# Four column groups of the first block's input projection as plain float32 products with raw weights

## The chip, the cores and the metric

The kernel runs on one core of one Trainium2 chip. The metric is device time in microseconds (us) of one execution; lower is better. TensorE (PE) multiplies, with its weight loads listed apart as PEld; VectorE (DVE), ScalarE (ACT) and GpSimd (POOL) work on elements; SyncE (SP) issues most DMAs.

## The reference, cut to what matters

A sequence of 256 tokens with 1024 channels passes two layers of a first block and then two layers of a second block. The change touches the input projection of the first block:

```
for l in range(2):
    h = rmsnorm(x, norm_mix[l])
    proj = einsum('bsd,de->bse', h, w_in[l])          # 1024 x 3476, float32
    m_q, m_k, m_v, m_o, m_i, m_f, b_q, ..., n_g = split(proj)
    qk = silu(causal_conv(concat([m_q, m_k]), conv_qk[l]))
    y = concat([mlstm(...), moba(...), nsa(...)])     # three mixers of the tokens
    x = x + y @ w_out[l]
    x = x + square(relu(rmsnorm(x, norm_ffn[l]) @ w_ff1[l])) @ w_ff2[l]
```

The groups in question are m_q, m_k, m_v and m_o, 512 columns each: the inputs of the mLSTM mixer. Its two convolved inputs (m_q, m_k) are made in two halves of heads.

## The kernel before

All weights go through one stream (class `Stream`) in the order of their use. A unit is up to 1072 float32 values on each of 128 partitions, mostly 128 x 1024 (512 KB). SP loads it into one of four raw buffers. Then `conv` splits it: ACT copies raw to `whi` (float32r, L154), and POOL (every second unit) or DVE subtracts `wlo` = raw - whi (L156). Up to four units are split ahead of use. The activations are split alike: `xT` transposes x (L570), ACT writes `xh` (L576) and DVE `xl` (L579), both times the gain of the norm. A product is then three float32r matmuls in one PSUM bank, xh.whi + xh.wlo + xl.whi (`mm3`, L242 is the line of every `mm`).

The first block's projection of one layer runs in this order: a group of 268 columns, one of 128, one of 512, the compression weights, one of 520, and then the four groups of the change in the order "0o1v": the first halves of m_q and m_k ("0": two pairs of column blocks, weights stationary, 256 tokens moving, `wpair`), m_o ("o": tokens on partitions, 512 columns moving, `xchunk`), the second halves ("1"), and m_v ("v"). After a pair, `conv_tile` runs the causal convolution: one DVE multiplication (L1151), one ACT copy (L1035) and three DVE instructions (L1037) for each block of 128 columns.

Attention work runs beside the projections. Two lanes hold queues of generator tasks (NSA, MoBA, gates, later mLSTM). Each `mm` adds its modelled time to a counter; at each 1000 ns (`tick`) the weight stream is converted ahead and every lane makes one step. The order on each engine is then settled by the framework, which reorders instructions by a simulated timeline. The tasks' own matmuls (scores, P @ v) and transposes have plain float32 operands. When "1" is done, three ticks later `act_conv` applies the tanh set and queues the mLSTM tasks (`mlstm_task`), which run beside "v" and the first products with w_out. `outproj` takes the mixers' results in the order n, b, m0, m1.

At the end of the feed-forward part, `bound_half` adds the result to x for one half of the columns, transposes it and computes the next norm, while the held products of the other half still run. DVE lines that the prediction names belong to the attention tasks: L296 to L299 (rope), L811 to L814 (compression, `cmph`), L861 and L866 (gains of the NSA norm), L714 (copy of transposed probabilities), L1019 (gates), L1086 (the mLSTM output `w`).

Of the kernel before, what the change touches and what calls it, by code (L numbers as in the profile page):

```python
# [31 lines left out]
C_SB = 1152         # [s, t]: NEG where t <= s  # L32
C_TRI = 1280        # -1 where s' >= s
C_COS = 1408        # [2, 16]
C_SIN = 1440        # [2, 16]
C_CM = 1472         # compressed mask, additive [2, 16]
C_CM1 = 1504        # compressed mask, 0/1 [2, 16]
C_SUM = 1536        # row sums of the hi/lo pairs, 16 wide
C_KBD = 1552        # [32, 2]
C_VBD = 1554        # [64, 4]  # L40
C_S8 = 1558         # [40, 8]
C_MONE = 1566       # -1
C_ONE = 1567        # 1
C_DUP = 1568        # [r, c] = 1 where c = r modulo 64
C_N = 1696
# [69 lines left out]
class Stream:  # L115
    """The weights in the order of use: loaded, then split into two float32r parts."""
    RAW = 4
    BUFS = 5
    SUB = 1072
# [9 lines left out]
    def add(self, a, b, *dmas):  # L129
        self.units.append((a, b, dmas))  # L130

    def load(self):
        u = self.n_load
        self.n_load += 1
        a, b, dmas = self.units[u]
        t = self.k.wraw.tile([128, self.SUB], F32, name="raw", tag="raw")
        v = t[:, :a * b].rearrange("p (a b) -> p a b", a=a)
        for f, src in dmas:
            self.k.nc.sync.dma_start(f(v), src)
        self.raw[u] = v  # L140

    def conv(self):
# [5 lines left out]
        a, b, _ = self.units[u]  # L148
        v = self.raw.pop(u)
        hi = self.k.wsub.tile([128, self.SUB], F32R, name="whi", tag="whi")  # L150
# [22 lines left out]
class K:  # L173
# [37 lines left out]
    def steps(self):  # L211
        """One step of every lane, and what was put off until now."""
# [44 lines left out]
    def rstd(self, out, ssq, inv, n, tag, lane="", ssq2=None, token=None):  # L257
        """out = 1 / sqrt(ssq * inv + EPS), or with two parts of the mean: 1 / sqrt(ssq + ssq2 + EPS)."""
# [30 lines left out]
    def rope(self, x, nh, lane, eng=None):  # L289
        """x [128, 2, nh, >=16] in place on the first 16."""  # L290
# [11 lines left out]
    def setup(self):  # L302
        nc, A = self.nc, self.A
        self.x = self.cst.tile([128, 2, DM], F32, name="x")
        cp = self.cst.tile([128, C_N], F32, name="cp")
        self.cp = cp
        wz = self.cst.tile([128, 512], BF16, name="wz")
# [18 lines left out]
        self.xl = self.cst.tile([128, KT, 256], F32R, name="xl")  # L326
        self.rs = self.cst.tile([128, 2], F32, name="rs")
# [5 lines left out]
        nc.sync.dma_start(cp[:, 128:], A["consts"][:, 128:])  # L333
# [6 lines left out]
    def setup2(self):  # L340
        nc, A, cp = self.nc, self.A, self.cp
        st = self.big.tile([128, 2048], F32, name="qkT", tag="qkT")
        cr = st[:96, 0:128]
        for i, n in enumerate(("norm_ffn", "pre_norm_2")):
# [25 lines left out]
        nc.vector.tensor_copy(self.msb, cp[:, C_SB:C_SB + 128])  # L370
        self.s8 = self.cst.tile([128, 8], F32R, name="s8")
        nc.scalar.activation(self.s8, cp[:, C_S8:C_S8 + 8], AF.Copy)
        self.tri = self.cst.tile([128, 129], F32R, name="tri")
        nc.scalar.activation(self.tri[:, 0:128], cp[:, C_TRI:C_TRI + 128], AF.Copy)
        nc.scalar.activation(self.tri[:, 128:129], cp[:, C_MONE:C_MONE + 1], AF.Copy)
        self.zero = self.cst.tile([8, 256], F32, name="zero")
        nc.gpsimd.memset(self.zero, 0.0)
        self.cumr = self.cst.tile([128, 384], F32R, name="cumr")
        nc.gpsimd.memset(self.cumr.bitcast(F32), 0.0)
        self.negM = self.cst.tile([64, 256], F32R, name="negM")  # L380
        nc.gpsimd.memset(self.negM.bitcast(F32), 0.0)
# [16 lines left out]
    def plan(self):  # L398
# [4 lines left out]
        def cols(t, l, width, c0, n, kts):  # L403
            for k0 in range(0, KT, kts):
                w.add(kts, n, (same, dram(t, (l * DM + k0 * 128) * width + c0, [[width, 128], [128 * width, kts], [1, n]])))

        def xch(t, l, width, c0, n):
            cols(t, l, width, c0, n, 2)
# [5 lines left out]
        for l in range(2):  # L414
            t, W = A["w_in"], 3476
            cols(t, l, W, 3208, 268, 2 if l == 0 else 4)
# [8 lines left out]
            for step in self.ORDER:  # L425
                if step == "o":
                    xch(t, l, W, 1536, 512)
                elif step == "v":
                    xch(t, l, W, 1024, 512)
                else:  # L430
                    for c in (0, 512):
                        cols(t, l, W, c + 256 * int(step), 256, 4)
# [34 lines left out]
    def xchunk(self, n, evac, first=None, pieces=None, both=False):  # L467
        """x @ n columns, tokens on partitions; first: the flag of the norm before, whose halves may still be due."""
# [36 lines left out]
    def wpair(self, ps, first=None):  # L505
        """ps[j] [128, 256] = (x @ weight columns)^T for two blocks of 128 columns."""
        k = 0
        while k < KT:
# [976 lines left out]
```

## Time and profile before

| what | value |
|---|---|
| time, median of 3 runs | 1159.69 us (1158.9 to 1159.82) |
| span of the profiled execution, first to last instruction | 1157.1 us |
| mean granted clock of TensorE | 0.986 of 2.4 GHz |
| busy: PE, PEld | 1110.5 us, 964.6 us |
| busy: DVE, ACT, POOL | 683.7, 639.4, 453.7 us |
| ACT copies raw to whi | 328, 344.4 us |
| subtractions on POOL, on DVE | 164, 408.8 us; 164, 214.4 us |

The profile is one execution. Its own time on the device stands nowhere beside its span; the median of the runs is 2.6 us longer than the span, which is what lies around it. Busy times are sums of instructions, and they overlap between engines; a long busy sum of an engine costs time only where another engine waits for it.

### The profile page before, as it was taken

The page shows a single profiled execution, that of the slowest core. Times are in us where ns is not written, and L with a number is a line of the kernel's source. Part 1 is how long each engine was busy: PE and PEld are TensorE (multiplying, and loading weights), DVE is VectorE, ACT ScalarE, POOL GpSimd, SP SyncE. Part 2 cuts the span into 40 slices and gives each one's busy share as a digit, 9 for nine tenths or more (in the row PEclk, how much of TensorE's full clock was granted, in tenths as well). Part 3 has the DMA queues.
Part 4 walks back from the last instruction along what each step waited for, and adds up shares of the span by engine and source line. Part 5 has one row for each costly group of instructions (what it writes and reads, how often), then busy time and mean ns, then how long its engine had stood idle before and what let it go on. Part 6 is the DMA issues. An engine that isn't in the chain of part 4 may idle for free.

```text
span 1157.1 us, 18183 instructions
## 1 busy us (share of the span) xinstructions
PE 1110.5 (96%) x6839; PEld 964.6 (83%) x6839; DVE 683.7 (59%) x1319; ACT 639.4 (55%) x1213; POOL 453.7 (39%) x234
## 2 busy tenths in 40 slices
PE   6988989999999999999999999999999999999997
PEld 4876878998998787878989898797997877979986
DVE  3897866545456896766555655474364386623543
ACT  4665546544556555546454545666655466676452
POOL 4652323444443442323444443434442243353421
PEclk8998999999999998999999999999999999999999
DMA  7743244656565633344665555644353346444530
GB/s 224 236 138 100 98 130 146 200 182 195 180 198 157 202 110 104 116 128 155 193 192 188 184 184 162 186 127 145 109 185 108 127 146 185 146 126 113 180 127 36
DMA packets 115511, 177.88 MB, mean 154 GB/s; under 512 B 5808, under 2 KB 75776, under 8 KB 115424
## 3 DMA queue, kind: packets, MB, share of 16 engines
q1 hardware_dynamic: 114368, 174.14, 47.9%
q0 software_dynamic: 832, 2.51, 0.9%
q8 instruction: 53, 0.87, 0.3%
q14 instruction: 34, 0.28, 0.1%
q10 hardware_dynamic: 224, 0.08, 0.0%
HBM read 175.66 MB, written 1.05 MB: 153 GB/s over the span
## 4 chain that ended last, share of the span: by engine, by line
PE 50%; DVE 3%; ACT 1%; issue 0%; DVEq 0%
PE g L242 34%; PE a L242 14%; PE a L710 1%; DVE wlo L156 1%; PE a L754 0%; DVE mc L272 0%; ACT w L1220 0%; ACT whi L154 0%; DVE rsm L271 0%; PE a L1247 0%; DVE rsm L263 0%; DVE w L1229 0%; DVE gate L1402 0%; DVE gate L1377 0%; ACT L275 0%
## 5 line engine op out<-in xcount | busy, mean ns | idle before, releaser
L156 POOL TENSOR_TENSOR wlo<-raw,whi 128x1024 fp32r<-128x1024 f32 (+2 forms) x164 | 408.8, 2493 | 637.5 <-ACT whi L154 519.8
L154 ACT ACTIVATE whi<-raw 128x1024 fp32r<-128x1024 f32 (+2 forms) x328 | 344.4, 1054 | 295.6 <-PE g L242 185.8
L156 DVE TENSOR_TENSOR wlo<-raw,whi 128x1024 fp32r<-128x1024 f32 (+2 forms) x164 | 214.4, 1308 | 156.0 <-ACT whi L154 144.9
L242 PE MATMUL g<-whi,xl 128*128 128x512 f32 (+3 forms) x480 | 174.8, 368 | 1.6 <-DVE xl L579 1.6
L242 PE MATMUL g<-wlo,xh 128*128 128x512 f32 (+3 forms) x480 | 175.3, 367 | 1.0 <-POOL wlo L156 0.7
L242 PE MATMUL g<-whi,xh 128*128 128x512 f32 (+2 forms) x480 | 174.3, 368 | 0.5 <-ACT xh L576 0.5
L242 PE MATMUL g<-whi,mh 128*128 128x512 f32 x416 | 163.7, 396 | 0.7 <-ACT mh L755 0.7
L242 PE MATMUL g<-wlo,mh 128*128 128x512 f32 x416 | 164.4, 395 | 0.0
L242 PE MATMUL g<-whi,ml 128*128 128x512 f32 x416 | 160.1, 394 | 0.3 <-DVE ml L756 0.3
L242 PE MATMUL a<-xl,whi 128*128 128x256 f32 x480 | 134.8, 281 | 0.0
L242 PE MATMUL a<-xh,wlo 128*128 128x256 f32 x480 | 134.5, 280 | 0.0
L242 PE MATMUL a<-xh,whi 128*128 128x256 f32 x480 | 134.4, 280 | 0.0
L242 PE MATMUL g<-xl,whi 128*128 128x256 f32 x432 | 123.8, 288 | 1.7 <-DVE xl L579 1.7
L242 PE MATMUL g<-xh,wlo 128*128 128x256 f32 x432 | 123.4, 286 | 0.8 <-DVE wlo L156 0.8
L242 PE MATMUL g<-xh,whi 128*128 128x256 f32 x432 | 123.3, 288 | 0.7 <-ACT xh L576 0.4
L678 DVE TENSOR_TENSOR ml<-e,mh 128x256 fp32r<-128x256 f32 x64 | 91.1, 1441 | 31.1 <-ACT mh L677 31.1
L242 PEld LDWEIGHTS g<-whi,xl 128*128 128x128 f32 x480 | 91.9, 192 | 17.8 <-issue 2.9
L242 PEld LDWEIGHTS g<-wlo,xh 128*128 128x128 f32 x480 | 92.0, 192 | 16.6 <-issue 2.2
L242 PEld LDWEIGHTS g<-whi,xh 128*128 128x128 f32 x480 | 91.5, 192 | 13.5 <-ACT xh L576 0.7
L242 PEld LDWEIGHTS g<-whi,ml 128*128 128x128 f32 x416 | 77.7, 188 | 17.6 <-DVE ml L756 0.5
L242 PEld LDWEIGHTS g<-whi,mh 128*128 128x128 f32 x416 | 78.1, 188 | 17.0 <-ACT mh L755 0.9
L242 PEld LDWEIGHTS a<-xl,whi 128*128 128x128 f32 x480 | 90.2, 188 | 1.3
(323 smaller groups left out, 1757.4 us busy)
## 6 DMA issues: line engine op xcount, KB each, us to landing
raw<-in_w_in_dram SPq DMA_DIRECT2D x130, 512.0 KB, 3.7
raw<-in_w_ff_dram SPq DMA_DIRECT2D x128, 512.0 KB, 3.9
raw<-in_w_out_dram SPq DMA_DIRECT2D x40, 512.0 KB, 3.3
raw<-in_w_in_dram SPq DMA_DIRECT2D x16, 520.0 KB, 4.2
raw<-in_cmp_w_dram SPq DMA_DIRECT2D x16, 256.0 KB, 3.8
raw<-in_w_in_dram SPq DMA_DIRECT2D x4, 268.0 KB, 12.2
raw<-in_w_in_dram SPq DMA_DIRECT2D x2, 536.0 KB, 3.9
x<-in_x_dram SPq DMA_DIRECT2D x4, 256.0 KB, 7.6
```

The costliest lines, as they stand in the source:

```text
L154: nc.scalar.activation(hv, v, AF.Copy)
L156: e.tensor_tensor(lv, v, hv.bitcast(F32), ALU.subtract)
L242: i = self.nc.tensor.matmul(out, l, r, start=st, stop=sp, skip_group_check=skip)
L678: nc.vector.tensor_tensor(ml[:, j], u, mh[:, j].bitcast(F32), ALU.subtract)
L710: nc.tensor.transpose(ps[:, b * 128:(b + 1) * 128], P[:, i, b * 128:(b + 1) * 128], self.ident)
```

## The change

A unit of the four groups is marked `whole`. `conv` passes it on raw, with no ACT copy and no subtraction, and its raw buffer stays occupied until PE has read it. Its products are single matmuls of plain float32 operands: the raw weights and a new operand `x32`, the transposed x times the gain in float32, which `xT` writes with extra ACT copies at the two norms that precede the first block's layers (flags "i" and "g0"). The counter of the ticks takes n / 0.6 ns (512 columns) or 430 ns (256) for such a product.

x32 needs 8 KB on each partition. To make room, units are at most 1040 values (the 268-column group of layer 1 becomes four units instead of two), 265 columns of the constants are loaded by a DMA on ACT's queue into a buffer used once (`once`), the rows of zeros are taken from other tiles (`zero`, `negM`), the warm-up operand `wz` and one lane's `sph` use other buffers' tags.

```diff
 class Stream:
-    SUB = 1072
+    SUB = 1040
...
     def conv(self):
...
+        if whole:
+            self.out[u] = (v, None)
+            return
...
 def setup(self):
-        cp = self.cst.tile([128, C_N], F32, name="cp")
+        cp = self.cst.tile([128, C_KEEP], F32, name="cp")
-        wz = self.cst.tile([128, 512], BF16, name="wz")
+        wz = self.big.tile([128, 512], BF16, name="y", tag="y", bufs=3)
+        self.x32 = self.cst.tile([128, KT, 256], F32, name="x32")
-        nc.sync.dma_start(cp[:, 128:], A["consts"][:, 128:])
+        nc.sync.dma_start(cp[:, 128:], A["consts"][:, 128:C_KEEP])
...
 def setup2(self):
+        once = st[:, 1280:1280 + C_N - C_KEEP]
+        nc.scalar.dma_start(once, A["consts"][:, C_KEEP:])
-        nc.vector.tensor_copy(self.msb, cp[:, C_SB:C_SB + 128])
+        nc.vector.tensor_copy(self.msb, once[C_SB])
-        self.zero = self.cst.tile([8, 256], F32, name="zero")
-        nc.gpsimd.memset(self.zero, 0.0)
+        self.zero = cp[:8, C_CZC + 128:C_CZC + 129].to_broadcast([8, 256])
-        self.negM = self.cst.tile([64, 256], F32R, name="negM")
-        nc.gpsimd.memset(self.negM.bitcast(F32), 0.0)
+        self.negM = self.cumr[0:64, 0:256]
...
 def plan(self):
-            cols(t, l, W, 3208, 268, 2 if l == 0 else 4)
+            cols(t, l, W, 3208, 268, 2)
                 if step == "o":
-                    xch(t, l, W, 1536, 512)
+                    xch(t, l, W, 1536, 512, True)
                 elif step == "v":
-                    xch(t, l, W, 1024, 512)
+                    xch(t, l, W, 1024, 512, True)
                 else:
                     for c in (0, 512):
-                        cols(t, l, W, c + 256 * int(step), 256, 4)
+                        cols(t, l, W, c + 256 * int(step), 256, 4, True)
...
 def xpart(self, ps, pieces, subs, tt, kts):
+                    if lv is None:
+                        self.mm(p[:, :n], self.x32[:, k, tt * 128:(tt + 1) * 128], hv[:, j, o:o + n], k == 0, k == last,
+                                n / 0.6)
+                        continue
...
 def wpair(self, ps, first=None):
+                    if lv is None:
+                        self.mm(p, hv[:, i, c], self.x32[:, k + i], k + i == 0, k + i == KT - 1, 430.0)
+                        continue
...
-    def xT(self, lane, kts, tts, gcol):
+    def xT(self, lane, kts, tts, gcol, whole=False):
...
+        if whole:
+            for a, kt in enumerate(kts):
+                nc.scalar.activation(self.x32[:, kt, t], ps[:, a * w:(a + 1) * w], AF.Copy, scale=gcol[:, kt:kt + 1])
...
 def sb_task(self, lane, l, half, qkT, vs, gg):
-            hi = lane.sb("sph", 384, dt=F32R, bufs=2)
+            hi = (self.sc.tile([128, 384], F32R, name="sph", tag=("nsA", "nkT")[i % 2]) if lane.name == "0"
+                  else lane.sb("sph", 384, dt=F32R, bufs=2))
```

## Rows read from the trace of the kernel before

**Rows 1.** The page's first part: engine, busy us (share of the span), instructions.

```profile
PE 1110.5 (96%) x6839; PEld 964.6 (83%) x6839; DVE 683.7 (59%) x1319; ACT 639.4 (55%) x1213; POOL 453.7 (39%) x234
```

**Rows 2.** Engine sums by stretch: length, busy us of each engine, PEclk, DMA share, GB/s.

```profile
62.00:88.00 26.00, 25.66 (x173) 22.55 (x174) 23.34 (x65) 16.17 (x41) 15.11 (x11) 0.93 0.45 142
88.00:105.00 17.00, 13.47 (x62) 10.45 (x61) 13.12 (x26) 6.03 (x12) 4.45 (x4) 0.80 0.31 94
105.00:148.00 43.00, 43.00 (x286) 36.92 (x286) 32.48 (x79) 26.72 (x59) 13.00 (x8) 1.00 0.32 104
...
408.00:435.00 27.00, 27.00 (x178) 23.58 (x177) 25.37 (x69) 16.43 (x41) 12.16 (x8) 0.94 0.35 101
435.00:446.00 11.00, 9.03 (x35) 6.96 (x35) 8.32 (x14) 3.59 (x8) 2.28 (x4) 0.69 0.30 94
446.00:490.00 44.00, 44.00 (x295) 37.62 (x293) 29.70 (x79) 28.09 (x60) 13.62 (x7) 1.00 0.31 108
```

**Rows 3.** PE's waits over the whole span: total us, times, longest us.

```profile
PE a L242 <- DVE P L714: 5.1, 2, 3.1
PE a L754 <- DVE w L1086: 4.6, 4, 2.3
...
PE a L242 <- DVE cmph L813: 3.8, 1, 3.8
...
PE a L883 <- DVE rsc L825: 1.9, 1, 1.9
PE a L883 <- DVE w L861: 1.7, 1, 1.7
```

**Rows 4.** Timeline of DVE in three stretches: start, us, engine, line, operation.

```profile
54.53 2.70 DVE L866 TENSOR_TENSOR kn<-kn,rp 128x128 f32<-128x128 f32 x2
...
57.61 2.38 DVE L296 TENSOR_TENSOR w<-kn,cp 128x64 f32<-128x64 f32 x1
...
402.11 0.21 DVE L296 TENSOR_TENSOR w<-kn,cp 128x64 f32<-128x64 f32 x1
...
434.94 2.38 DVE L1019 TENSOR_TENSOR negM<-w,negM 4x256 fp32r<-4x256 f32 x1
```

**Rows 5.** Timeline of POOL in the same stretches.

```profile
57.35 2.56 POOL L156 TENSOR_TENSOR wlo<-raw,whi 128x1024 fp32r<-128x1024 f32 x1 [0.47 <-DVE cmpe L811]
...
433.66 3.38 POOL L156 TENSOR_TENSOR wlo<-raw,whi 128x1024 fp32r<-128x1024 f32 x1 [3.03 <-issue]
```

**Rows 6.** Groups by form from 62 to 148 us: busy us, mean ns, idle before.

```profile
L156 POOL TENSOR_TENSOR wlo<-raw,whi 128x1024 fp32r<-128x1024 f32 x8 | 22.5, 2807 | 38.3 <-ACT whi L154 21.9 <-PE a L242 11.1 <-PE a L883 5.3
L242 PE MATMUL g<-xh,wlo 128*128 128x256 f32 x64 | 18.6, 290 | 0.0
...
L154 ACT ACTIVATE whi<-raw 128x1024 fp32r<-128x1024 f32 x16 | 16.8, 1052 | 7.7 <-PE g L242 7.1 <-issue 0.6
L242 PE MATMUL g<-whi,xh 128*128 128x512 f32 x32 | 13.5, 422 | 0.0
```

**Rows 7.** Timeline of PE: the first and last of twelve, and of ten, split matmuls.

```profile
104.14 0.39 PE L242 MATMUL g<-whi,xh 128*128 128x512 f32 x1
...
106.68 0.40 PE L242 MATMUL g<-whi,xl 128*128 128x512 f32 x1
...
109.09 0.28 PE L242 MATMUL g<-xh,whi 128*128 128x256 f32 x1
...
110.15 0.28 PE L242 MATMUL g<-xh,whi 128*128 128x256 f32 x1
```

**Rows 8.** Timeline of PE: the first and last of four plain records' starts.

```profile
153.09 0.38 PE L242 MATMUL a<-qkT 128*128 128x256 f32 x1
...
153.73 0.49 PE L242 MATMUL a<-qkT 128*128 128x256 f32 x2
```

**Rows 9.** Groups by form on ACT, from 0 to 30 us.

```profile
L576 ACT ACTIVATE xh<-a,colm 128x256 fp32r<-128x256 f32 x8 | 3.2, 469 | 11.4 <-PE a L570 11.4
```

**Rows 10.** DMA issues of the page: count, KB each, median us from issue to landing.

```profile
raw<-in_w_out_dram SPq DMA_DIRECT2D x40, 512.0 KB, 3.3
```

More of the change, by code (lines that the diff above doesn't have):

```diff
@@ L31 @@
 C_ML = 896
[L32 to L45, printed above, removed]
+C_COS = 1152
+C_SIN = 1184
+C_CM = 1216
+C_CM1 = 1248
+C_SUM = 1280
+C_KBD = 1296
+C_VBD = 1298
+C_ONE = 1302
+C_DUP = 1303
+C_KEEP = 1432
+C_SB = 1432
+C_TRI = 1560
+C_MONE = 1688
+C_S8 = 1689
+C_N = 1697
 def consts():
@@ L127, in __init__, with add @@
         self.out = {}
-    def add(self, a, b, *dmas):
-        self.units.append((a, b, dmas))
+    def add(self, a, b, *dmas, whole=False):
+        self.units.append((a, b, dmas, whole))
     def load(self):
@@ L134, in load @@
         self.n_load += 1
-        a, b, dmas = self.units[u]
+        a, b, dmas, _ = self.units[u]
         t = self.k.wraw.tile([128, self.SUB], F32, name="raw", tag="raw")
@@ L147, in conv @@
             self.load()
-        a, b, _ = self.units[u]
+        a, b, _, whole = self.units[u]
         v = self.raw.pop(u)
+        if whole:
+            self.out[u] = (v, None)
+            return
         hi = self.k.wsub.tile([128, self.SUB], F32R, name="whi", tag="whi")
@@ L343, in setup2 @@
         cr = st[:96, 0:128]
+        once = st[:, 1280:1280 + C_N - C_KEEP]
+        nc.scalar.dma_start(once, A["consts"][:, C_KEEP:])
+        once = {c: once[:, c - C_KEEP:c - C_KEEP + n] for c, n in ((C_SB, 128), (C_TRI, 128), (C_MONE, 1), (C_S8, 8))}
         for i, n in enumerate(("norm_ffn", "pre_norm_2")):
@@ L369, in setup2 @@
         self.msb = self.cst.tile([128, 128], BF16, name="msb")
-        nc.vector.tensor_copy(self.msb, cp[:, C_SB:C_SB + 128])
+        nc.vector.tensor_copy(self.msb, once[C_SB])
         self.s8 = self.cst.tile([128, 8], F32R, name="s8")
-        nc.scalar.activation(self.s8, cp[:, C_S8:C_S8 + 8], AF.Copy)
+        nc.scalar.activation(self.s8, once[C_S8], AF.Copy)
         self.tri = self.cst.tile([128, 129], F32R, name="tri")
-        nc.scalar.activation(self.tri[:, 0:128], cp[:, C_TRI:C_TRI + 128], AF.Copy)
-        nc.scalar.activation(self.tri[:, 128:129], cp[:, C_MONE:C_MONE + 1], AF.Copy)
-        self.zero = self.cst.tile([8, 256], F32, name="zero")
-        nc.gpsimd.memset(self.zero, 0.0)
+        nc.scalar.activation(self.tri[:, 0:128], once[C_TRI], AF.Copy)
+        nc.scalar.activation(self.tri[:, 128:129], once[C_MONE], AF.Copy)
+        self.zero = cp[:8, C_CZC + 128:C_CZC + 129].to_broadcast([8, 256])
         self.cumr = self.cst.tile([128, 384], F32R, name="cumr")
         nc.gpsimd.memset(self.cumr.bitcast(F32), 0.0)
-        self.negM = self.cst.tile([64, 256], F32R, name="negM")
-        nc.gpsimd.memset(self.negM.bitcast(F32), 0.0)
+        self.negM = self.cumr[0:64, 0:256]
         lt = st[:, 512:1024]
@@ L401, in plan, with cols, xch @@
         same = lambda v: v
-        def cols(t, l, width, c0, n, kts):
+        def cols(t, l, width, c0, n, kts, whole=False):
             for k0 in range(0, KT, kts):
-                w.add(kts, n, (same, dram(t, (l * DM + k0 * 128) * width + c0, [[width, 128], [128 * width, kts], [1, n]])))
-        def xch(t, l, width, c0, n):
-            cols(t, l, width, c0, n, 2)
+                w.add(kts, n, (same, dram(t, (l * DM + k0 * 128) * width + c0, [[width, 128], [128 * width, kts], [1, n]])),
+                      whole=whole)
+        def xch(t, l, width, c0, n, whole=False):
+            cols(t, l, width, c0, n, 2, whole)
         def rowsw(t, l, rows, r0):
@@ L602, in bound_half @@
         for q in range(2):
-            self.xT(self.lanes[q], (h * 4 + 2 * q, h * 4 + 2 * q + 1), (0, 1), gcol)
+            self.xT(self.lanes[q], (h * 4 + 2 * q, h * 4 + 2 * q + 1), (0, 1), gcol, flag in ("i", "g0"))
         self.done.add(flag + "x%d" % h)
```

## The prediction

> **What bounds the kernel now.** I read the table of engines first: TensorE (PE) is busy 96% of the span [rows 1]. So time spent on PE counts almost in full, and what matters of the other engines is only where PE waits for one of them. The changed groups lie in the first block, twice (layer 0 about 62 to 148 us, layer 1 about 408 to 490 us), so I asked for engine sums by stretch next [rows 2]. The reader is to see that PE is busy there, that its granted clock is not: 0.93 and 0.80 in layer 0, 0.94 and 0.69 in layer 1, where 1.0 is the 2.4 GHz level and the shortfall is time at the 1.2 GHz level. The rest of both stages (105 to 148, 446 to 490 us) ran at 1.0 with PE busy throughout. The lost clock is (1 - 0.93) x 26 + (1 - 0.80) x 17 + (1 - 0.94) x 27 + (1 - 0.69) x 11 = 1.8 + 3.4 + 1.6 + 3.4 = 10.2 us. The list of PE's waits says what stands before each of these stretches [rows 3]: the five waits for VectorE (DVE) at cmph, P (two), rsc and w (L861) sum to 3.8 + 5.1 + 1.9 + 1.7 = 12.5 us, and they are the whole of PE's long idle time in the two stages and the 520-column group before them. The timelines of DVE and GpSimd (POOL) then say why DVE was late [rows 4, 5]. Six DVE instructions ahead of the waits, the first at 54.53 and the last at 434.94 (five waits, two of the six before cmph), took 2 us more than elsewhere: L296 at 57.61 took 2.38 us and on the same shape 0.21 us at 402.11. Each ran beside a POOL subtraction wlo <- raw, whi and ended about when that ended: 57.61 + 2.38 = 59.99 against 57.35 + 2.56 = 59.91, and 434.94 + 2.38 = 437.32 against 433.66 + 3.38 = 437.04. These POOL instructions split the units of the four groups that are to change, up to four units ahead of use.
>
> **What the change removes and adds on PE.** Per layer the split products of these groups are 192 matmuls of 256 columns and 96 of 512 (three operand pairs of 64 and 32, in the grouped view) [rows 6]. At full clock twelve 512-column ones start from 104.14 to 106.68, 0.231 us apart, and ten 256-column ones from 109.09 to 110.15, 0.118 us apart [rows 7]. So 192 x 0.1178 + 96 x 0.2309 = 44.8 us go. A plain float32 product appears as two matmul records. The attention products of 256 columns on 128 rows show it: four such records start from 153.09 to 153.73, 0.213 us apart, twice the time per column of a split matmul [rows 8]. No plain matmul of 512 columns is in the trace; from below it is twice the 256-column record (0.427 us), from above that times the split matmuls' own excess over columns / 2.4 GHz (0.2309 / 0.2133), 0.462 us. I take the lower, since the plain record of 256 columns shows no such excess. Added: 64 x 2 x 0.2133 + 32 x 2 x 0.4267 = 54.6 us. The balance is +9.8 us a layer, **+19.6 us** in both (+24 at the upper bound). All of it is on the path: PE has no other slack.
>
> The Trainium skill (TensorE: Matmul & The Clock Gate, section "Back-to-back issue gap") puts a full-clock matmul at columns / 2.4 GHz + 2.5 ns. By that the removed products would be 41.7 us and the whole forecast 6 us higher, 1170; the rows give 0.118 and 0.231 us where it says 0.109 and 0.216, and the rows decide.
>
> **What it takes from the other engines.** Sixteen units a layer are no longer converted: 16 ScalarE (ACT) copies, and 16 subtractions, half of them on POOL at 2.8 us [rows 6]. None of that time counts by itself; it counts through the five waits. If no POOL subtraction runs beside DVE's chain, the stretched instructions fall from about 2.4 us to a few tenths, so some 2 us leave each chain (twice that before cmph, with two stretched ones), as much as each wait lasted but the one of 3.1 us. With the waits the low clock behind them goes. At stake are 12.5 + 10.2 = 22.7 us; the bounds are 0 (other work queues up in their place, PE's order being written anew by the planner) and 22.7. I take three quarters, **-17.0 us**: the cause is seen on all the waits, but POOL keeps work of its own and DVE is well filled, at 23.3 of 26 and 25.4 of 27 us [rows 2]. The stall goes next to the end of the attention chain.
>
> The Trainium skill (SBUF — State Buffer, section "SBUF: two separate sides") says that DVE instructions with two SBUF inputs and GpSimd instructions that read SBUF take a shared pair of ports as an exclusive lock, and the loser stands still until the other is done. The stretched rows end with the POOL instruction, which agrees. By that rule every stretch goes with its POOL instruction and 22.7 us come back: 1158, no change. It is the third case below.
>
> **What moves.** The v group is the last projection, and the mLSTM steps run beside it. Sixteen products grow from 3 x 0.231 to 2 x 0.427, so that group lasts 2.6 us longer and hides that much more of the chain whose end PE now waits for, 4.6 us in both layers, as the four waits for w of L1086 [rows 3]. Bounds 0 and 4.6, I take half: **-2.3 us**.
>
> The new operand x32 costs 8 ACT copies at each of two norms; xh from the same bank is the nearest row, 0.47 us, so 16 x 0.47 = 7.5 us of ACT [rows 9]. At the start ACT waits 11.4 us ahead of these copies for the transposes of x, and the first four fall in there; the other four (1.9 us) precede the conversion of weights. At the norm between the layers the held feed-forward products cover the first four, and I leave 1.0 us. **+2.9 us**, bounds 0 and 7.5.
>
> A raw unit now holds its buffer until PE has used it, not until it is copied, so loads run three units ahead. Each unit lasts 4 x 0.853 = 3.4 us of PE, three are 10 us, and a 512 KB unit of w_out lands in 3.3 us [rows 10]; inside the groups nothing waits. At the hand-over w_out must land, be copied (1.05 us) and subtracted (2.8 us) [rows 6], 7.2 us against those 10 us, if SP's queue, ACT and POOL take it at once. Bounds 0 and 14 us (no cover, twice), taken **+1.0 us**.
>
> At nothing I put: the constants on ACT's queue (135 KB that leave SP's, hidden while x lands; 0.9 us at 512 KB in 3.3 us if not), the mask copies behind them, the shared zero rows, the smaller raw buffers with two more units in layer 1 (hidden under feed-forward products; one more copy of 1.05 us of ACT if not), and sph in other buffers of the same number.
>
> Sum: 19.6 + 2.9 + 1.0 - 17.0 - 2.3 = +4.2 us. The span of the profiled execution is 1157.1 us; the median of the runs, 1159.7, leaves 2.6 us around it. So 1157.1 + 2.6 + 4.2 = **1163.9 us**.
>
> **Rivals.**
> - *Forecast*: the extra passes cost 20 us and most of it comes back from waits and clock. 1163.9, own range 1162 to 1171.
> - *Little comes back*: DVE's chain, nearly full, still comes last, PE waits elsewhere, and the clock falls as before. With a quarter of 22.7 and nothing at mLSTM: 19.6 + 3.9 - 5.7 = +17.8, 1177.5. For it: DVE's 25.4 of 27 us. Against it: the long waits all follow stretched instructions, not a full queue alone.
> - *All waits go*: 19.6 + 3.9 - 2.3 - 22.7 = -1.5, 1158.2, no change that can be measured.
> - *Faster*: DVE's relief carries through to the mLSTM chain, whose 4.6 us go too: 19.6 + 3.9 - 22.7 - 4.6 = -3.8, 1155.9. It decides once over 25.8 us come back of 27.3. Against it: the w_out subtractions beside mLSTM stay on POOL.
>
> That a plain product needs no more PE time than a split one is excluded by 2 x 0.213 against 3 x 0.118 us.
>
> **Numbers.** Within 0.2% (2.3 us) of 1159.7 a measurement can't tell from no change. Chances: forecast 0.42, little comes back 0.20 (slower 0.62); all waits go 0.20 (same); faster 0.18. The range leaves about a tenth outside at either end: below, the faster case with the edges at nothing (-7.7, 1152) is cut at 1154; above, the second case with the hand-over's stalls (over 1179) is cut there.
>
> **What would show it.** PE records of the four groups: two per product, 0.213 and 0.427 us apart, some 20 us more PE time in the stages; slower than 0.427 makes the first term too small. No POOL subtraction from 54 to 148 us but those of the 520 group, DVE's L296, L861, L866, L1019, L1037 at 0.2 to 0.5 us, PE's waits for P, cmph and rsc gone, and the clock at 1.0 in both stages. If the clock still falls there, the second case holds. If PE waits for raw or w_out data, my reading of the loads was wrong. A pause at 17 to 21 or 363 to 367 us behind xh would be the price of x32.

## The result, and the profile after

The changed kernel took 1176.22 us (median of 4 runs, 1174.92 to 1177.2) against 1159.3 us for the kernel before (4 runs, 1158.86 to 1159.82): a ratio of 1.0143, 95% interval 1.0129 to 1.0157, some 17 us slower. Two of run 5's ten executions took 2214.7 and 3706.5 us and are left out of its time. The span of its profiled execution is 1175.3 us, 18.2 us longer than the 1157.1 us before, at a mean granted clock of 0.983.

The direction and the range held. The central number, 1163.9 us, was 12 us too low. The time is that of the second case (1177.5, "little comes back"), but not by that case's mechanism: inside the four groups waits and lost clock were gone, and the loss arose in two other places that the sum had priced at +1.0 and at nothing.

The page's table of engines (compare [rows 1]) gives PE 16 us more; PE idles 48.9 us of the span, 46.6 before, so over the whole kernel no waiting was saved. The list of PE's waits (compare [rows 3]) has other names than before:

```profile
PE 1126.4 (96%) x6647; PEld 953.9 (81%) x6647; DVE 642.0 (55%) x1304; ACT 617.4 (53%) x1199; POOL 405.4 (34%) x217
```

```profile
PE a L772 <- DVE w L1104: 8.1, 3, 4.9
PE g L247 <- DVE y L814: 5.0, 1, 5.0
...
PE a L901 <- DVE w L304: 3.4, 1, 3.4
...
PE g L247 <- ACT mh L773: 2.5, 1, 2.5
```

The waits for P, cmph and rsc are gone. L1104 and L304 are the old L1086 and rope; `y` (compression) had cost 1.0 us, and `mh` (the transposed mixer result) did not stand among the long waits before.

To see where the time went, I cut both executions at the same events, read from the timelines, always at the start of the instruction: the last `xh` of the first norm, the last evacuation (copy out of PSUM) of the 520 group, that of v, the last addition to x after the output product and after the feed-forward part. The table gives the lengths in us; later runs stand beside them.

| stretch | before | after | v split | no x32 | two units | before, DVE |
|---|---|---|---|---|---|---|
| to the last xh, layer 0 | 18.7 | 19.9 | 19.6 | 20.9 | 19.5 | 18.8 |
| first groups to 520, layer 0 | 48.0 | 42.1 | 42.2 | 43.6 | 42.7 | 41.6 |
| the four groups, layer 0 | 80.8 | 78.5 | 77.1 | 78.6 | 79.8 | 74.5 |
| output product, layer 0 | 33.9 | **45.6** | 33.8 | 43.5 | 44.1 | 35.6 |
| feed-forward, layer 0 | 181.8 | 181.9 | 181.9 | 182.0 | 181.8 | 181.8 |
| norm and first groups, layer 1 | 45.5 | **59.4** | 55.0 | 55.1 | 41.8 | 40.0 |
| the four groups, layer 1 | 79.8 | 80.8 | 78.1 | 80.1 | 80.3 | 72.0 |
| output product, layer 1 | 31.9 | 29.7 | 31.9 | 30.3 | 41.0 | 37.9 |
| the rest | 636.8 | 637.3 | 637.6 | 637.6 | 636.3 | 636.6 |

Two stretches lose 11.7 + 13.9 = 25.6 us. The groups that were changed lose nothing: -5.9 - 2.3 + 1.0 = -7.2 us with the 520 group before them. The engine sums of the four groups and of the two lossy stretches show where PE idles and where the clock is low, first after, then before:

```profile
62.00:140.50 78.50, 78.50 (x383) 55.20 (x382) 43.86 (x136) 32.38 (x88) 9.74 (x13) 1.00 0.38 111
140.50:186.10 45.60, 37.79 (x163) 29.87 (x161) 25.01 (x59) 17.58 (x40) 11.86 (x5) 0.85 0.40 127
368.00:427.40 59.40, 48.95 (x307) 42.59 (x306) 37.56 (x101) 34.29 (x85) 19.43 (x10) 0.91 0.43 125
427.40:508.20 80.80, 80.80 (x387) 56.71 (x386) 48.04 (x131) 31.62 (x77) 8.04 (x12) 1.00 0.37 110
```

```profile
66.70:147.50 80.80, 77.27 (x495) 65.25 (x494) 65.31 (x157) 46.12 (x104) 31.75 (x20) 0.96 0.33 103
147.50:181.40 33.90, 30.83 (x152) 24.25 (x150) 21.43 (x53) 15.42 (x35) 10.16 (x4) 1.00 0.41 130
363.20:408.70 45.50, 40.69 (x282) 36.70 (x283) 36.70 (x74) 28.01 (x60) 21.28 (x11) 0.99 0.58 176
408.70:488.50 79.80, 77.83 (x493) 66.44 (x493) 62.55 (x158) 45.91 (x104) 27.60 (x18) 0.94 0.32 105
```

In the groups PE is busy in every microsecond at full clock, where it had idled 3.5 and 2.0 us at 0.96 and 0.94; DVE fell from 65 to 44 us and from 63 to 48. In the two other stretches PE idles 7.8 and 10.5 us (3.1 and 4.8 before), and the clock is down to 0.85 and 0.91.

The counts of PE's records show that work moved as well. The products have 96 records fewer in each layer, but the groups lost 112 and 106, and the two lossy stretches hold 11 and 25 more than before. So a part of what the groups gained and the other stretches lost, some 4 to 5 us as I estimate from the steps between those records, is attention and mLSTM work that PE did at another time.

The plain products cost what was forecast. In the timeline of PE (first start, length of the row), six 256-column records in a row, and six of 512:

```profile
63.78 1.46 PE L247 MATMUL g<-x,raw 128*128 128x256 f32 x6
...
82.03 2.74 PE L247 MATMUL g<-raw,x 128*128 128x512 f32 x6
```

A row runs from the first start to the last end: 1.46 us are five steps of 0.216 and one record of 0.38, 2.74 us five of 0.429 and one of 0.60 (mean records of the grouped view: 0.383 and 0.595). So a layer's products take 128 x 0.216 + 64 x 0.429 = 55.1 us, 10.3 more than the 44.8 that the prediction reckoned for those removed (forecast 9.8). Both are steps of uninterrupted rows; PE's busy time in both layers together rose by 15.9 us, not by 20.6.

**The output product, layer 0.** ACT's timeline stands still for w_out near the end of v and behind it (v's evacuations begin at 138.72 and 140.48):

```profile
137.75 1.06 ACT L159 ACTIVATE whi<-raw 128x1024 fp32r<-128x1024 f32 x1 [4.16 <-DMA raw<-in_w_out_dram]
...
144.13 1.06 ACT L159 ACTIVATE whi<-raw 128x1024 fp32r<-128x1024 f32 x1 [1.80 <-DMA raw<-in_w_out_dram]
145.10 1.07 ACT L773 ACTIVATE mh<-a 128x512 fp32r<-128x512 f32 x2
```

`mh` is queued behind the last of these copies, and PE waits for it; then the clock is down, as PE's records and the engine sums show:

```profile
145.73 0.79 PE L247 MATMUL g<-whi,mh 128*128 128x512 f32 x1 [2.47 <-ACT mh L773]
...
146.75 0.63 PE L247 MATMUL g<-whi,mh 128*128 128x512 f32 x1
147.18 0.63 PE L247 MATMUL g<-wlo,mh 128*128 128x512 f32 x1
```

```profile
145.00:152.00 7.00, 6.27 (x17) 5.01 (x17) 2.24 (x5) 1.99 (x5) 2.38 (x1) 0.52 0.56 191
152.00:169.00 17.00, 13.07 (x69) 10.80 (x69) 11.09 (x32) 7.58 (x25) 4.72 (x2) 0.99 0.32 93
169.00:176.00 7.00, 6.02 (x18) 4.54 (x19) 3.07 (x12) 0.82 (x2) 0.00 (x0) 0.53 0.25 75
```

Split matmuls step by 0.43 us there, at 0.231 elsewhere [rows 7]: the 1.2 GHz level. The mLSTM scores lie in that stretch too, its output `w` comes late, PE waits 4.9 us for it and the clock falls again. Two stretches of 7 us at about half clock cost some 3.3 us each. Two DVE instructions of this chain are stretched beside POOL (L1093 with 1.80 us at 160.88, L275 with 2.15 us for two at 166.53), but the kernel before had two such there as well (2.13 and 2.35 us), so they are no part of the difference.

**The norm, layer 1.** ACT's timeline from the last `xh` (ends 372.63) to the Ln and Exp of the norm (`rsx`), L598 being the new x32 copies:

```profile
373.71 1.60 ACT L598 ACTIVATE x<-a,colm 128x256 f32<-128x256 f32 x4
375.14 1.12 ACT L159 ACTIVATE whi<-raw 128x1024 fp32r<-128x1024 f32 x1
376.09 0.90 ACT L598 ACTIVATE x<-a,colm 128x256 f32<-128x256 f32 x2
376.80 1.14 ACT L159 ACTIVATE whi<-raw 128x1024 fp32r<-128x1024 f32 x1
377.75 0.92 ACT L598 ACTIVATE x<-a,colm 128x256 f32<-128x256 f32 x2
378.46 0.30 ACT L290 ACTIVATE rsx<-rsx 128x2 f32<-128x2 f32 x1
378.56 2.09 ACT L159 ACTIVATE whi<-raw 128x1024 fp32r<-128x1024 f32 x2
380.45 0.29 ACT L290 ACTIVATE rsx<-rsx 128x2 f32<-128x2 f32 x1
```

Four conversions stand ahead of the second `rsx`, which ends 8.1 us behind the last `xh`. In the kernel before it was one conversion and 3.0 us (last `xh` ends 367.23), and DVE's step behind it (L270, now L275) was not stretched:

```profile
368.67 0.20 ACT L285 ACTIVATE rsx<-rsx 128x2 f32<-128x2 f32 x1 [0.23 <-DVE rsx L265]
369.12 1.06 ACT L154 ACTIVATE whi<-raw 128x1024 fp32r<-128x1024 f32 x1 [0.24 <-PE g L242]
370.08 0.19 ACT L285 ACTIVATE rsx<-rsx 128x2 f32<-128x2 f32 x1
```

```profile
371.36 0.15 DVE L270 TENSOR_TENSOR rsx<-rsx 128x2 f32<-128x2 f32 x1
```

In the changed kernel that step runs beside POOL; so do two rope instructions later:

```profile
381.47 2.39 DVE L275 TENSOR_TENSOR rsx<-rsx 128x2 f32<-128x2 f32 x1
...
401.66 2.46 DVE L302 TENSOR_TENSOR w<-kn,cp 128x32 f32<-128x32 f32 x1
404.04 2.44 DVE L303 TENSOR_TENSOR w<-kn,cp 128x32 f32<-128x32 f32 x1
```

```profile
380.73 3.11 POOL L161 TENSOR_TENSOR wlo<-raw,whi 128x1024 fp32r<-128x1024 f32 x1 [0.27 <-ACT whi L159]
...
400.83 5.60 POOL L161 TENSOR_TENSOR wlo<-raw,whi 128x1040 fp32r<-128x1040 f32 x2 [7.31 <-ACT whi L159]
```

381.47 + 2.39 = 383.86 against 380.73 + 3.11 = 383.84: the stretching of [rows 4, 5], moved to another place. The waits for `y` (5.0) and the rope's `w` (3.4) follow, and behind them 3.4 and 6.8 us at a granted clock of 0.50 (397.5 to 400.9 and 407.8 to 414.6 us). Across the runs the wait of 5.0 us for `y` goes with the four small units: every run below that has them shows it (4.9 in run 6), also run 9, where no POOL subtraction is near, and run 3, without x32; in the kernel before, run 4, run 7, run 8 and run 12, which have two units, PE waits 1.0 us or less for `y`.

### The profile page after: what moved, and what is told of

It is laid out like the page before. It is cut to its first block, busy times and chain, and to the rows that moved or that the text cites. A ratio compares the mean times of both kernels' runs of the same rounds, so it can differ in the third digit from the quotient of the medians.

```text
span 1175.3 us, 17689 instructions
## 1 busy us (share of the span) xinstructions
PE 1126.4 (96%) x6647; PEld 953.9 (81%) x6647; DVE 642.0 (55%) x1304; ACT 617.4 (53%) x1199; POOL 405.4 (34%) x217
## 3 DMA queue, kind: packets, MB, share of 16 engines
HBM read 175.66 MB, written 1.05 MB: 150 GB/s over the span
## 4 chain that ended last, share of the span: by engine, by line
PE 88%; DVE 6%; ACT 2%; DMA 2%; issue 1%; POOL 0%; SPq 0%; DVEq 0%; POOLq 0%; ACTq 0%
PE g L247 59%; PE a L247 25%; PE a L728 1%; DMA x<-in_x_dram 1%; DVE wlo L161 1%; ACT whi L159 1%; PE a L772 1%; DMA raw<-in_w_out_dram 1%; DVE mc L277 1%; PE a L585 0%; DVE rsm L276 0%; ACT w L1238 0%; PE a L1265 0%; DVE rsm L268 0%; DVE x L617 0%
## 5 line engine op out<-in xcount | busy, mean ns | idle before, releaser
L161 POOL TENSOR_TENSOR wlo<-raw,whi 128x1024 fp32r<-128x1024 f32 (+2 forms) x149 | 364.3, 2446 | 592.4 <-ACT whi L159 517.7
L159 ACT ACTIVATE whi<-raw 128x1024 fp32r<-128x1024 f32 (+2 forms) x298 | 311.9, 1051 | 289.6 <-PE g L247 167.9
L161 DVE TENSOR_TENSOR wlo<-raw,whi 128x1024 fp32r<-128x1024 f32 (+2 forms) x149 | 194.8, 1308 | 161.6 <-ACT whi L159 149.2
L247 PE MATMUL g<-wlo,xh 128*128 128x512 f32 (+3 forms) x416 | 149.4, 360 | 1.6 <-POOL wlo L161 1.6
L247 PE MATMUL g<-whi,xl 128*128 128x512 f32 (+3 forms) x416 | 147.9, 360 | 1.6 <-DVE xl L594 1.6
L247 PE MATMUL g<-whi,xh 128*128 128x512 f32 (+3 forms) x416 | 149.0, 363 | 0.0
L247 PEld LDWEIGHTS g<-whi,mh 128*128 128x128 f32 x416 | 79.3, 191 | 19.9 <-ACT mh L773 3.0
L247 PEld LDWEIGHTS g<-whi,ml 128*128 128x128 f32 x416 | 78.0, 188 | 18.2 <-issue 0.2
L247 PEld LDWEIGHTS g<-wlo,mh 128*128 128x128 f32 x416 | 79.3, 191 | 16.3 <-DVE P L1071 0.2
L247 PEld LDWEIGHTS a<-xh,whi 128*128 128x128 f32 x480 | 90.8, 189 | 1.3
L247 PEld LDWEIGHTS g<-wlo,xh 128*128 128x128 f32 x416 | 79.8, 192 | 14.4 <-issue 2.5
L247 PEld LDWEIGHTS g<-whi,xl 128*128 128x128 f32 x416 | 79.5, 192 | 13.6 <-DVE xl L594 2.0
L247 PEld LDWEIGHTS a<-xh,wlo 128*128 128x128 f32 x480 | 90.1, 188 | 0.1
```

The costliest lines, as they stand in the source:

```text
L159: nc.scalar.activation(hv, v, AF.Copy)
L161: e.tensor_tensor(lv, v, hv.bitcast(F32), ALU.subtract)
L247: i = self.nc.tensor.matmul(out, l, r, start=st, stop=sp, skip_group_check=skip)
```

## The experiments

Each run was timed beside the kernel before on the same chip, and ratios are to that. The kernel before took 1159.3 us beside the changed kernel, 1160.8 beside runs 1 to 4, 1160.4 beside runs 5 to 8 and 1160.9 beside runs 9 to 12, so differences of times across these groups are good to some 1.5 us. "Theory" in the expectations is what I held at that time.

**1. x32 on POOL.** The sum xh + xl, made by POOL behind the norm, in place of ACT's copies.

```
-                nc.scalar.activation(self.x32[:, kt, t], ps[:, a * w:(a + 1) * w], AF.Copy, scale=gcol[:, kt:kt + 1])
...
+                nc.gpsimd.tensor_tensor(self.x32[:, kt:kt + 2], self.xh[:, kt:kt + 2].bitcast(F32),
+                                        self.xl[:, kt:kt + 2].bitcast(F32), ALU.add)
```

> The changed kernel, but x32 is no longer copied by ACT from PSUM: POOL adds xh + xl in SBUF after the norm (x32 is then exact to the rounding of the split halves). Theory A (the plain passes are paid back inside the four groups; what is lost is lost outside them, about 14 us of it ahead of the groups in layer 1, where the eight copies of x32 stand before the norm's Ln and Exp in ACT's queue): those copies gone, 1161 to 1167 us, the 5 us wait of the compression products for y gone or under 2 us, the clock at 1.0 there. Rival B (the loss is the plain passes, and what differs outside the groups is chance of the planner's order): 1173 to 1179 us.

Measured: 1178.1 us, ratio 1.0154 (1.0128 to 1.018). The norm's stretch fell to 54.4 us, but the first groups of layer 0 rose to 47.4: the work moved, and the time did not fall. The wait for `y` is still 5.0 us. Theory A's 1161 to 1167 missed; the time lies in rival B's range, though B's reason (the loss is the plain passes) doesn't fit the table.

**2. The layout alone.** The changed kernel, x32 written, but all four groups split in three products again (three lines, of which one is shown).

```
-                    xch(t, l, W, 1536, 512, True)
+                    xch(t, l, W, 1536, 512)
```

> The changed kernel with no unit marked whole: the four groups are split products again, everything else of the change stays (x32 written by ACT and read by nobody, smaller buffers, constants on ACT's queue). Theory A: the copies of x32 cost here what they cost in the changed kernel, so slower than before by 5 to 15 us, 1164 to 1174 us, with the norm factor of layer 1 ready 4 us or more later after xh than before. Rival B: no more than 2 us from the kernel before, 1157 to 1162 us.

Measured: 1166.1 us, ratio 1.0051 (1.0034 to 1.0069), in theory A's range. So what lies around the plain products (smaller buffers, four units, x32) costs some 5 us by itself, and the plain units some 10. The output product of layer 0 is back at 34.0 us, the norm's stretch of layer 1 still at 56.8: the first loss belongs to the whole units, the second to the layout (x32 included).

**3. No x32.** The plain products read xh as float32, so the low half of x is left out in them; no extra copies (the same in `xpart`).

```
-                        self.mm(p, hv[:, i, c], self.x32[:, k + i], k + i == 0, k + i == KT - 1, 430.0)
+                        self.mm(p, hv[:, i, c], self.xh[:, k + i].bitcast(F32), k + i == 0, k + i == KT - 1, 430.0)
```

> The changed kernel without x32: the plain products read xh as float32 (the low half of x is left out of the four groups, so only the time counts). Theory A: like the run with x32 on POOL, 1161 to 1167 us, and the two within 2 us. Rival B: 1173 to 1179 us. If this is fast and the run with POOL is not, POOL's additions block DVE instead.

Measured: 1173.12 us, ratio 1.0105 (1.0087 to 1.0123). The copies are worth 3.1 us by the medians, 4.4 by the ratios, against the 2.9 forecast. The time lies at the edge of rival B's range, and not within 2 us of run 1 as theory A had it. The norm's stretch falls by 4.3 us only, to 55.1, with the same 5.0 us wait for `y`: x32 is the smaller part of that loss.

**4. The kernel before, its four groups' subtractions on DVE.** No product changes; the 16 units a layer are still split, but none by POOL (their three lines of the plan carry a flag, not shown).

```
-        e = nc.gpsimd if u % self.POOL == 1 else nc.vector
+        e = nc.gpsimd if u % self.POOL == 1 and not dve else nc.vector
```

> The kernel before, its four groups split as ever, but all their subtractions on DVE and none on POOL (8 of 16 units a layer move, some 10 us of DVE a layer). If POOL's subtractions stretch DVE's chain (theory of the prediction): the five waits of 12.5 us fall under 5 us, the clock stays at 1.0 in both stages, 1142 to 1154 us. If DVE is simply full there, the added 10 us a layer make it later: 1162 to 1175 us, the waits longer.

Measured: **1140.73 us**, ratio 0.9828 (0.9813 to 0.9843), 20 us faster than the kernel before, 1 us below the expected range. The waits for P, cmph, rsc and w of L861 are gone. Engine sums of the two stages, and DVE's L1019:

```profile
60.30:134.80 74.50, 73.14 (x479) 62.53 (x477) 64.86 (x163) 45.73 (x104) 15.10 (x16) 0.98 0.42 127
408.20:480.20 72.00, 71.26 (x444) 60.86 (x445) 55.55 (x145) 41.90 (x96) 16.85 (x13) 1.00 0.36 111
```

```profile
425.39 0.41 DVE L1019 TENSOR_TENSOR negM<-w,negM 4x256 fp32r<-4x256 f32 x1
```

DVE does eight more subtractions a layer and is as busy as before (64.9 against 65.3 us, 55.6 against 62.6), because its own instructions no longer stretch: L1019 takes 0.41 us, 2.38 before [rows 4]. That is the prediction's cause for the waits, shown with the products untouched. "DVE nearly full", the reason for the second case, falls. A rival, that the units are simply ready earlier on the faster DVE, does not fit: once the first norm was done, PE waited for `wlo` 1.6 us in the whole kernel, and none of the five waits was for it.

**5. v split.** The changed kernel, with the last group (v) in three products again.

```
-                    xch(t, l, W, 1024, 512, True)
+                    xch(t, l, W, 1024, 512)
```

> The changed kernel with only the last of the four groups (v) split into three products again; o and the two 256-column pairs stay plain, x32 and the layout stay. A (the loss at the output product is the hand-over: whole units hold their buffers until PE has used them, so the w_out units behind them land and are split too late): the stretch from the end of v to the end of the output product falls from 45.6 us in the changed kernel to 37 us or less in layer 0, ACT no longer waits there for a transfer of w_out, and the time is 1162 to 1170 us. Rival B (the stretch is long because the mLSTM chain loses cover or because the order of the lanes is a different one, whoever holds the buffers): the stretch stays at 42 us or more, the time 1172 to 1180 us.

Measured: 1160.5 us, ratio 1.0005 (0.999 to 1.0019): 16 us less than with v plain, and no difference from the kernel before. The stretch went theory A's way, and the time came out 1.5 us below its range. The output product of layer 0 takes 33.8 us at full clock, and the long wait is gone:

```profile
138.90:172.70 33.80, 31.16 (x157) 24.98 (x155) 21.27 (x57) 16.63 (x38) 9.82 (x5) 1.00 0.47 144
```

```profile
PE a L772 <- DVE w L1104: 1.4, 2, 1.2
PE a L247 <- DVE P L1071: 1.2, 1, 1.2
```

Of the 18.0 us between the two spans, 11.8 lie there. The four groups are 1.4 and 2.7 us shorter (16 products of v in three matmuls, not two records, are 16 x (2 x 0.429 - 3 x 0.231) = 2.6 us a layer), the norm's stretch 4.4 us (clock 0.97, not 0.91), and layer 1's output product is 2.2 us longer.

**6. Six raw buffers,** in run 3's kernel (low half of x left out), with the unused tile gone.

```
-    RAW = 4
+    RAW = 6
```

> The kernel of the run without x32 (the plain products read xh as float32, so the low half of x is left out in them; 1173.1 us), with six raw buffers in place of four and the unused x32 tile gone. A (hand-over): two more buffers let w_out land earlier, the stretch at the output product of layer 0 falls from 43.5 us to 37 us or less, the time is 1162 to 1168 us. Rival B (buffers are not what holds it): the stretch stays above 41 us, the time 1170 to 1176 us.

Measured: 1170.57 us, ratio 1.0085 (1.0069 to 1.0101), 2.6 us less than run 3 (1.0105, 1.0087 to 1.0123: the intervals overlap). The wait for `mh` is gone, as the hand-over theory says, but theory A's times missed; the output product still takes 40.9 us, at 0.92 of the clock:

```profile
PE a L768 <- DVE w L1100: 4.9, 1, 4.9
PE a L768 <- DVE w L959: 0.7, 1, 0.7
```

So buffers held too long explain the wait for `mh` and at most some 2.6 us, not the whole loss. The mLSTM output still comes late behind a plain v: from v's second evacuation to the first `w` it takes 24.1 us here (139.93 to 164.01), 19.0 with v split (138.94 to 157.93), 28.7 in the changed kernel (140.48 to 169.22), 27.3 in run 3.

The timelines show one thing that goes with it: how far the chain had come when v ended. DVE's first step for each of the four heads (`P<-a,acol,cp` 128x256, L1069 in the changed kernel) needs no v. Before, two of the four ran ahead of v's second evacuation in either layer. In the changed kernel it was one in layer 0 (the others 3.5 to 12.1 us behind it) and all four in layer 1, where the first `w` came after 15.2 us (before: 16.4 and 18.2). In layer 0 of run 6 and with v split it was one as well, but the others came 2.4 to 7.4 and 1.2 to 5.8 us behind v. Why the lanes were behind in layer 0 no run shows.

**7. Two units in layer 1,** in run 3's kernel (low half of x left out): buffers of 1072 columns, the 268 group in two units as before, the unused tile gone.

```
-    SUB = 1040
+    SUB = 1072
...
-            cols(t, l, W, 3208, 268, 2)
+            cols(t, l, W, 3208, 268, 2 if l == 0 else 4)
```

> The kernel of the run without x32 (low half of x left out in the plain products; 1173.1 us), with raw buffers of 1072 columns again, so that layer 1's 268-column group goes in two units as in the kernel before, not in four. A (with four smaller units the later ones are split during the norm, where POOL's subtractions stretch the norm's instructions on DVE): the stretch from the first xh of layer 1 to the 520-column group falls from 55.1 us to 48 us or less (45.5 before), the time is 1162 to 1168 us. Rival B (the two more units cost nothing, the stretch is long for another reason, such as the units behind it): it stays above 52 us, the time 1170 to 1176 us.

Measured: 1169.28 us, ratio 1.0077 (1.006 to 1.0095). The stretch fell from 55.1 to 41.8 us, further than theory A said, at full clock. ACT's timeline from the last `xh` (ends 372.06) on:

```profile
373.51 0.20 ACT L290 ACTIVATE rsx<-rsx 128x2 f32<-128x2 f32 x1 [0.23 <-DVE rsx L270]
373.93 1.06 ACT L159 ACTIVATE whi<-raw 128x1024 fp32r<-128x1024 f32 x1 [0.22 <-PE g L247]
374.90 0.18 ACT L290 ACTIVATE rsx<-rsx 128x2 f32<-128x2 f32 x1
```

One conversion stands in the norm, not four. The look-ahead counts units, of whatever size (`BUFS` = 5: at a tick four units ahead of use, at most five not yet freed): with four small units fewer of the 1024-column units behind them are split before the norm begins. POOL's timelines show it, first in the changed kernel, then here:

```profile
362.67 1.36 POOL L161 TENSOR_TENSOR wlo<-raw,whi 128x536 fp32r<-128x536 f32 x1 [3.70 <-ACT whi L159]
```

```profile
362.51 2.40 POOL L161 TENSOR_TENSOR wlo<-raw,whi 128x1024 fp32r<-128x1024 f32 x1 [2.44 <-issue]
```

That is the mechanism of the second loss. But the whole run gained 3.8 us (3 by the ratios), not 13.3: now layer 1's output product took 41.0 us (run 3: 30.3), with waits of 2.6 us for `mh` and 3.9 us for `w` and a clock of 0.88: the first loss in the other layer. There one head's first step ran ahead of v's end, where in run 3 it was four. The time for theory A missed, its place held.

**8. The kernel before, all first-block subtractions of w_in and the compression weights on DVE,** with the flag of run 4 on these lines too.

```
-            cols(t, l, W, 3080, 128, 8)
-            xch(t, l, W, 2568, 512)
+            cols(t, l, W, 3080, 128, 8, True)
+            xch(t, l, W, 2568, 512, True)
```

> The kernel before, with every subtraction of the first block's input projection and of the compression weights on DVE, none on POOL (the run with only the four groups' units there took 1140.7 us). A (each POOL subtraction beside DVE's chain costs more than it saves, in the norm and the 520-column group too): 1132 to 1139 us, and no DVE instruction of the norm between the layers above 2 us. Rival B (DVE is the bound there once it takes these units as well: the units ahead of the norm come late): 1141 to 1152 us.

Measured: 1146.98 us, ratio 0.9884 (0.9865 to 0.9903), rival B's range. The groups grow shorter still (70.5, 71.4 us), the output products longer (43.0, 38.6); the norm's stretch of layer 1, where B saw the loss, is not longer (40.5, run 4: 40.0).

**9. The changed kernel, the same units ahead of the groups on DVE** (268, 128, 512, 520 columns and the compression weights).

```
-            xch(t, l, W, 2568, 512)
+            xch(t, l, W, 2568, 512, dve=True)
```

> The changed kernel, complete, with the subtractions of the units ahead of the four groups (268, 128, 512 columns, the compression weights, 520 columns; both layers) on DVE, none on POOL. A (the loss between the layers is POOL's subtractions stretching the norm and key instructions on DVE, L275, L302 and L303 at 2.4 us each): these fall to 0.5 us or less, the stretch from the first xh of layer 1 to the end of the 520-column group falls from 59.4 to 50 us or less, the time is 1160 to 1168 us. Rival B (the x32 copies and the later conversions delay the norm, whoever subtracts): the stretch stays above 55 us, the time 1171 to 1178 us.

Measured: 1175.71 us, ratio 1.0129 (1.0113 to 1.0144). L275, L302 and L303 fall, and the stretch with them, from 59.4 to 52.3 us:

```profile
385.30 0.15 DVE L275 TENSOR_TENSOR rsx<-rsx 128x2 f32<-128x2 f32 x1
...
404.86 0.19 DVE L302 TENSOR_TENSOR w<-kn,cp 128x32 f32<-128x32 f32 x1
404.96 0.19 DVE L303 TENSOR_TENSOR w<-kn,cp 128x32 f32<-128x32 f32 x1
```

But three subtractions now stand ahead of L275 on DVE itself, the 5.0 us wait for `y` stays, and layer 0 gets one of 4.0 us for `y` that it had not. The time is B's; the stretch lies between the two. With POOL's subtractions on DVE it is 7.1 us shorter, of the 13.9 lost there, but about as much is lost in other places.

**10. Runs 5 and 9 together,** v's subtractions on DVE (run 9's edit stands beside the line shown).

```
-                    xch(t, l, W, 1024, 512, True)
+                    xch(t, l, W, 1024, 512, dve=True)
```

> The run before this one and the run with v split, together: o and the two 256-column pairs plain, v split with its subtractions on DVE, the units ahead of the groups on DVE. A (the two losses are separate and add up: 15 us at the output product, 10 to 15 us between the layers): 1145 to 1153 us. Rival B (both are one loss that moves along with the order): 1156 to 1163 us, as with v split alone.

Measured: 1169.39 us, ratio 1.0073 (1.0058 to 1.0088), slower than run 5 alone. Both theories missed; the losses do not add up. PE waits 8.7 us for `y`, 3.6 of them in layer 0, where run 9's edit had brought such a wait too.

**11. The changed kernel, w_out of the first block on DVE.**

```
-                rowsw(A["w_out"], l, DM, r)
+                rowsw(A["w_out"], l, DM, r, True)
```

> The changed kernel, complete, with the subtractions of the first block's eight w_out units on DVE in both layers, none on POOL. A (POOL's w_out subtraction stretches the end of the mLSTM chain, L275 at 2.15 us, and PE's wait there draws the half clock after it): the stretch at the output product of layer 0 falls from 45.6 us to 41 us or less, the time is 1168 to 1173 us. Rival B (that place is held by the late units alone, and four more subtractions of 1.2 us on DVE are in the chain's way): it stays at 44 us or more, the time 1174 to 1181 us.

Measured: 1172.43 us, ratio 1.0102 (1.0085 to 1.0119), 3.8 us less. The output product of layer 0 fell to 42.4 us, not to 41; L275 was still at 2.15 us beside POOL's next unit, and PE still waited 4.9 us for `w`. It does not tell the two theories apart.

**12. Run 4 and w_out on DVE,** the edits of runs 4 and 11 together.

> The kernel before with the subtractions of the four groups and of w_out on DVE, none on POOL (the groups alone gave 1140.7 us). A (the same stretching costs time at the output product): 1134 to 1139 us. Rival B (the chain there has slack, or DVE's added subtractions take what they give): 1140 to 1145 us.

Measured: 1146.12 us, ratio 0.9872 (0.9857 to 0.9887), 5.4 us slower than run 4 and outside both ranges, on B's side. PE waits 4.9 us for the mLSTM output in layer 0 where run 4 waits 1.5. Run 4 is the fastest version found.

## Why the prediction came out as it did

| step | forecast, us | measured, us |
|---|---|---|
| more PE passes | +19.6 | +20.6 by the records' steps |
| waits and clock in the groups and the 520 group | -17.0 | with the passes -7.2, so the remainder is some -28, or -23 with PE's busy time for the passes; 19.1 were at stake there (22.7 less 3.6 in layer 1's first groups), the rest is at least in part work that moved |
| x32 copies | +2.9 | +3.1 to +4.4 (run 3) |
| hand-over to w_out, with the cover for mLSTM | +1.0 - 2.3 | +11.7 in layer 0; -2.2 in layer 1, where seven records of w_out had moved ahead of v's second evacuation |
| two more units in layer 1 | 0 | +13.3 in its stretch (run 7 against run 3, without x32 in both); +3.8 in the whole time |

- **The passes** were right by the steps, from the nearest row [rows 8] taken at twice for 512 columns. ("Twice the time per column of a split matmul" reads those rows too high: 0.213 against 0.118 us is 1.81 times.)
- **The waits** were right in cause and were gone in the groups; the three quarters were too cautious there. Run 4 shows the cause by itself. Over the whole kernel nothing of them was saved: PE idles 2.3 us more than before.
- **"+1.0, the hand-over"** was mis-sized. The sum compared 10 us of look-ahead with 7.2 us of landing and conversion and saw slack. It left out ACT's queue: a copy that waits for w_out holds up `mh` (the prediction had named PE waiting for w_out as the sign; here ACT waits, and PE behind it), and the wait is followed by the lower clock and a later mLSTM chain, for which PE waits again. Run 6 sizes the buffers' part at some 2.6 us of the 11.7. The loss hit one layer of two, and in run 7 both.
- **"-2.3, v hides more of the mLSTM chain"** failed in both layers: PE waits 4.9 and 3.2 us for `w`, 2.1 and 2.5 before. (The output product of layer 1 is 2.2 us shorter since seven of w_out's records run earlier, not since PE waits less.) The sum took it that a longer v hides more of the chain, whatever the lanes had begun by then; the steps that need v begin only when it ends. Run 5 shows the size of this and the hand-over together. What beyond the buffers makes the chain 5 us longer behind a plain v (run 6 against run 5) stays open: 1.9 us are L275 beside POOL in run 6 (2.14 us for two, 0.23 in run 5, which has another stretched instruction of 1.26 us in its place), the rest goes with the later start.
- **"At nothing: two more units in layer 1 (one more copy of 1.05 us)"** was a step that failed outright. It counted the added instructions, not the limit of five units that they use up: what is no longer split ahead is split inside the norm. The pause behind `xh` that the prediction named as a price of x32 came (8.1 us, 3.0 before), but for the larger part from this.

Two errors in opposite directions stood in the sum: some 11 us more than forecast came off the groups (the remainder above), some 23 us more were lost outside. That the time still fell into the range was luck as far as the mechanism goes. The rule from the Trainium skill that the prediction weighed (SBUF — State Buffer, section "SBUF: two separate sides": of a DVE instruction with two SBUF inputs and a GpSimd instruction that reads SBUF, one stands still while the other holds the shared ports) agrees with what runs 4 and 9 show: with no POOL subtraction beside them L275, L302, L303 and L1019 take 0.15 to 0.41 us, not 2.4. The case "all waits go" was met inside the groups; new waits elsewhere made the time another.

What is not settled: how much of the time hangs on which instruction happens to meet which. Run 2 has the products of the kernel before, and its layer 1 groups took 70.7 us, not 79.8, without an edit to them; run 7 lost in layer 1 what it had gained. What decides how far the mLSTM chain has come when v ends is not known, and with it the larger part of the first loss. A version with v split, two units in layer 1 and no other edit was not run.

## What to carry to other kernels

When a stream of weights has a limit in units, price a change of unit size by what is then no longer ready in time, not by the instructions added. When a buffer is held longer, look at the in-order queue of the engine that waits for the next load, and at who stands behind it. When a profile shows tiny VectorE instructions at 2.4 us beside a GpSimd elementwise operation, try first to move that operation, and only where such instructions are waited for: here it gave 20 us (run 4), 13 or 14 when more units were moved (runs 8 and 12), where saving the conversions altogether at the price of more matmul time made the kernel 17 us slower.

## What was not expected of the hardware

- A full-width plain float32 product of 512 columns is two records 0.429 us apart, 256 columns 0.216 (at a granted clock of 1.0): within 1.3% of the attention products' 0.213 [rows 8], and 512 columns take no more than twice that.
- Eight more subtractions a layer on DVE did not lengthen its busy time, since they removed the stretching of others; but w_out's four more a layer cost some 5 us (run 12). Which engine should subtract depends here on what runs beside it.
- PE idle times of 2.5 and 4.9 us were each followed by 7 us at a mean granted clock of 0.52 and 0.53: these waits cost their own length and some 3.3 us more. It is not the same for each: the 5.0 us wait for `y` was followed by 3.4 us at half clock, the 3.4 us wait for the rope's `w` by 6.8.
